# 32 bytes of padding in front of the ring of weight parts in a two-layer decoder trunk

## The chip, the cores and the metric

One core of one Trainium2 chip runs the whole program. The metric is the device time of one execution in microseconds; the kernel before was run three times, and the median counts. One further execution was taken with the hardware profiler, and all rows below come from it.

## What is computed

Two decoder layers over 256 positions of width 1024. Each layer is a mixer (latent attention in layer 0, three-branch sparse attention in layer 1), a residual with layer norm, and a PEER feed-forward with 16384 experts, again with residual and norm. Cut to the part that fills most of the time:

```python
def chunk(xc):                                   # PEER, 128 positions at a time
    q = (xc @ w_q).reshape(PEER_CHUNK, PEER_HEADS, 2, PEER_DK // 2)
    sc = jnp.einsum("thpd,hpnd->thpn", q, subkeys)
    s_half, i_half = lax.top_k(sc, PEER_TOPK)
    ...
    best, pos = lax.top_k(cand, PEER_TOPK)
    experts = jnp.take_along_axis(cand_idx, pos, axis=-1)
    g = jax.nn.softmax(best, axis=-1)
    a = jax.nn.gelu(jnp.einsum("thkd,td->thk", u[experts], xc), approximate=False)
    return jnp.einsum("thk,thkd->td", (g * a), v[experts])
```

The kernel does not gather `u`: it multiplies the activations with all 128 blocks of 128 experts, masks the result with the gates, and multiplies that with all of `v`. Only the last 64 positions (`GT`) gather their rows of `v`.

## The kernel before, in words

**Weight stream.** All weights pass through one stream (`plan`, L50) of parts of 128x1024 float32, one after the other: the latent-attention weights, then for each layer the 16 parts of `p_wq`, 128 parts of `p_u` and 128 of `p_v`, with the sparse-attention weights between the layers. A DMA from SyncE (L102 for two parts of `p_v`, L107 else) lands a part in one of four places of the tile `raw` (or, during `p_v`, in a second tile `spare` that lies where `hT` was). ScalarE rounds it to fp32r (L119, tile `hi`), VectorE subtracts (L130, tile `lo` = raw minus hi). `hi` and `lo` come from the pool `shl` of four buffers each: this is the ring of weight parts. TensorE then multiplies three products, hi with hi, hi with lo and lo with hi, so that the sum has float32's precision.

**The stages.** In the order of time:
- Latent attention (`mla`, L908). Its weights meet `hT` once (`proj_N`, L203, activations as the operand that is loaded into the array) and then `cT` (`proj_T`, L198, 256 columns streamed) and `oT` (`out_mm`, L1124, 512 columns of the weights streamed). Two of its eight output weights are kept in a pool `mkeep`, tile `keep`.
- PEER (`peer`, L442), once per layer. First 12 parts of `p_wq` by `proj_T`: the weights are loaded, 128x128 at a time, and `hT`, the transposed activations, is streamed, 256 columns at a time. Then 128 steps over `p_u` (`u_step`, L715): the first 40-odd are like `proj_T`, 24 matmuls of 256 columns. Once the routing is over, a step is "wide": 8 matmuls that stream 512 columns (both parts of `hT` side by side, for `hi`) and 8 of 256 (for `lo`), and every fourth step has 16 small fp16 matmuls from the one-hot tile `hot` beside it. Then 128 steps over `p_v` (`v_mm`, L813): here the masked activations `W` are loaded and the weight parts are streamed, 512 columns at a time, 10 matmuls a step. `W` lies in a tile of pool `r8` for steps 0 to 86 (`w_hi`, L766, takes `W[0]` as long as `late` is empty, and runs three steps ahead), and in the pool `late` (L847) for the rest.
- Sparse attention (`nsa`, L1246) between the two PEER parts: `hT` with weights by `proj_T`, and `oT` with weights by `out_mm`.

**Order.** The order of TensorE's work is written out by hand; a step's weights are prepared two steps ahead (`prep`, L157), so a step never waits for its DMA unless the ring falls behind.

**Places in memory.** Pools are stacked in the order in which they are opened (L352 to L358), and a tile takes a whole number of 32-byte units per partition. From the declared sizes follow the places of the tiles modulo 128 bytes:
- `const` starts at 0 and holds 2432 bytes and three small constants of 32 each, so `hT` (pool `pers`) starts at 96. Every further index of `hT` is a multiple of 128 bytes.
- `hT` has 16384 bytes, `small` 1088, so pool `r8` (`gb`, `hN`, the first `W`, `hot`) starts at 32; `raw`, behind its 16384 bytes, at 32; the ring `shl`, behind 16384 more, at 32. `spare` is where `hT` was, at 96.
- What is opened behind the ring: in `mla`, `cT` and `oT` are at 32 and `keep` at 64; in `peer`, the routing tiles, the gathered rows and the late `W` are at 32; in `nsa`, `oT` and its `keep` are at 96.

In this text the distance of a matmul is the place of the streamed operand minus that of the loaded one, modulo 128.

Of the kernel before, what the change touches and what calls it, by code (L numbers as in the profile page):

```python
# [12 lines left out]
F32 = mybir.dt.float32  # L13
# [11 lines left out]
P = 128  # L25
# [18 lines left out]
class Kern:  # L44
# [302 lines left out]
    def build(self):  # L347
        tc, nc, I = self.tc, self.nc, self.I
        with ExitStack() as es:
            es.enter_context(tc.manual_schedule())  # L350
            pool = lambda *a, **k: es.enter_context(tc.tile_pool(*a, **k))
# [3 lines left out]
            self.pr8 = pool(name="r8", bufs=2)  # L355
            self.nraw = 4
            self.raw4 = pool(name="sraw", bufs=1).tile([P, self.nraw, D], F32, name="raw")
            self.shl = pool(name="shl", bufs=4)  # L358
            self.pacc = pool(name="pacc", bufs=2, space=PSUM)
            self.pmm = pool(name="pmm", bufs=4, space=PSUM)  # L360
# [1303 lines left out]
```

## Time and profile before

| | us |
|---|---|
| runs | 1757.70, 1756.76, 1750.29 |
| median | 1756.76 |
| the profiled execution's own time | 1749.82 |
| its span, first to last instruction | 1748.0 |
| its mean granted TensorE clock | 0.994 |

The profile lists, by engine, busy time and shares of the span. The times that the trace gives to single matmuls overlap, since a matmul starts before the one before it has ended. What one matmul costs is read from the starts: a row of the timeline merges neighbours of one kind, and the start of the next row minus its own start, divided by its count, is the pace. The rows on which the prediction rests stand below the change.

### The profile page before, as it was taken

Reading aid. Unit: us, or ns where it says so; the run is one execution under the profiler, and the core shown is the slowest. Engines: PE = TensorE matmul, PEld = TensorE weight load, DVE = VectorE, ACT = ScalarE, POOL = GpSimd, SP = SyncE. Lnnn points to the kernel's source line nnn. Section 1 sums busy time; section 2 is a strip of 40 time slices with the busy share of each in tenths; the row PEclk is TensorE's granted clock in tenths of the full one; section 3 lists DMA queues with packets and bytes.
Section 4 is the critical chain, followed back from the end, with each engine's and each line's share of the span. In section 5 each row is a group of like instructions: output and inputs, shape, how many; then the busy total and the mean of one; then the engine's idle time right before and its main releaser. Section 6 shows DMA issues by size and latency. Waiting matters only on the chain.

```text
span 1748.0 us, 30707 instructions
## 1 busy us (share of the span) xinstructions
PE 1703.1 (97%) x10610; PEld 1478.1 (85%) x10610; DVE 1553.4 (89%) x3675; ACT 1042.9 (60%) x2267; POOL 481.4 (28%) x441
## 2 busy tenths in 40 slices
PE   7999999999999999999997999999999999999997
PEld 6879999888888788888785789998888888888886
DVE  5778988989998899999778789988899998999998
ACT  6646555766666555556466755556666666555554
POOL 2110002000001777761341210001000005777740
PEclk9999999999999999999999999999999999999999
DMA  7535667555556899999572265657555557999993
GB/s 246 169 128 195 193 204 261 186 178 181 187 183 251 309 391 370 367 360 332 179 268 67 95 206 176 205 184 275 176 181 186 184 183 290 401 383 369 361 363 110
DMA packets 118619, 416.66 MB, mean 238 GB/s; under 512 B 16032, under 2 KB 18112, under 8 KB 117376
## 3 DMA queue, kind: packets, MB, share of 16 engines
q1 hardware_dynamic: 88976, 322.60, 54.2%
q0 software_dynamic: 29488, 92.10, 14.1%
q8 instruction: 84, 1.38, 0.3%
q14 instruction: 71, 0.58, 0.1%
HBM read 400.49 MB, written 13.63 MB: 237 GB/s over the span
## 4 chain that ended last, share of the span: by engine, by line
PE 72%; issue 16%; DVE 6%; DMA 2%; ACT 2%; POOL 1%; SPq 0%; POOLq 0%; ACTq 0%; DVEq 0%
PE acc L196 36%; PE mm L196 35%; PE mm L223 1%; DVE lo L130 1%; DMA raw<-p_wq 1%; POOL actD L758 1%; DVE keep L130 1%; DMA xT<-xT 0%; POOL row L472 0%; ACT hi L119 0%; POOL gel L476 0%; DMA gel<-actD,gidx 0%; DVE gacc L486 0%; DVE W L774 0%; DMA actD<-gst 0%
## 5 line engine op out<-in xcount | busy, mean ns | idle before, releaser
L119 ACT CAST hi<-raw 128x1024 fp32r<-128x1024 f32 (+1 forms) x463 | 484.6, 1049 | 244.6 <-PE acc L196 99.8
L196 PE MATMUL mm<-hT,hi 128*128 128x256 f32 (+1 forms) x3360 | 612.8, 328 | 0.0
L130 DVE TENSOR_TENSOR lo<-raw,hi 128x1024 fp32r<-128x1024 f32 (+1 forms) x459 | 558.3, 1220 | 32.6 <-ACT hi L119 30.9
L196 PEld LDWEIGHTS mm<-hT,hi 128*128 128x128 f32 x3360 | 483.2, 188 | 46.3 <-issue 1.2
L196 PE MATMUL acc<-hi,W 128*128 128x512 f32 x1452 | 408.8, 390 | 0.0
L196 PEld LDWEIGHTS acc<-hi,W 128*128 128x128 f32 x1452 | 273.2, 188 | 57.0
L196 PEld LDWEIGHTS mm<-hT,lo 128*128 128x128 f32 x2376 | 306.7, 188 | 15.9
L196 PE MATMUL mm<-hT,lo 128*128 128x256 f32 x2376 | 320.0, 277 | 0.0
L196 PE MATMUL acc<-lo,W 128*128 128x512 f32 x968 | 299.6, 391 | 1.8 <-DVE lo L130 1.8
L758 POOL DMA_DIRECT2D actD<-gst x64 | 34.8, 544 | 783.9 <-ACT gst L756 783.9
L472 POOL DMA_INDIRECT row<-p_v,gidx x128 | 191.7, 1498 | 117.8 <-DVE gacc L486 79.9
L196 PEld LDWEIGHTS acc<-lo,W 128*128 128x128 f32 x968 | 181.7, 188 | 41.4 <-DVE lo L130 4.1
L119 ACT CAST hi<-spare 128x1024 fp32r<-128x1024 f32 x122 | 128.1, 1050 | 113.9 <-PE acc L196 100.8
L476 POOL DMA_INDIRECT gel<-actD,gidx x128 | 165.7, 1294 | 50.0 <-issue 36.6
L486 DVE SCALAR_TENSOR_TENSOR gacc<-row,gw,gacc 128x1024 f32<-128x1024 f32 x126 | 161.4, 1281 | 1.1
L130 DVE TENSOR_TENSOR lo<-spare,hi 128x1024 fp32r<-128x1024 f32 x122 | 148.8, 1220 | 5.4 <-ACT hi L119 4.5
L750 ACT ACTIVATE mm<-mm 128x192 f32<-128x192 f32 (+23 forms) x170 | 41.1, 242 | 122.4 <-DVE mm L748 122.4
L774 DVE TENSOR_TENSOR W<-A,W 128x128 fp32r<-128x128 f32 (+1 forms) x512 | 107.6, 252 | 1.8 <-ACT W L769 1.8
L748 DVE TENSOR_TENSOR mm<-mm,half 128x256 f32<-128x256 f32 x174 | 74.5, 428 | 15.4 <-ACT half L747 15.0
L769 ACT CAST W<-A 128x192 fp32r<-128x192 f32 x256 | 88.0, 345 | 0.0
L647 DVE SCALAR_TENSOR_TENSOR A<-acc,A 128x176 f32<-128x176 f32 (+16 forms) x268 | 56.1, 274 | 28.6 <-PE acc L196 25.6
L753 ACT ACTIVATE A<-mm 128x192 f32<-128x192 f32 (+23 forms) x244 | 67.3, 276 | 7.8 <-DVE mm L748 2.8
(275 smaller groups left out, 1759.1 us busy)
## 6 DMA issues: line engine op xcount, KB each, us to landing
raw<-p_u SPq DMA_DIRECT2D x256, 512.0 KB, 4.0
spare<-p_v SPq DMA_DIRECT2D x64, 1024.0 KB, 8.8
raw<-p_v SPq DMA_DIRECT2D x63, 1024.0 KB, 8.7
raw<-p_wq SPq DMA_DIRECT2D x32, 512.0 KB, 4.1
actD<-gst POOLq DMA_DIRECT2D x64, 128.0 KB, 3.9
raw<-b_wo SPq DMA_DIRECT2D x12, 512.0 KB, 3.8
raw<-a_wo SPq DMA_DIRECT2D x8, 512.0 KB, 4.6
raw<-s_wT SPq DMA_DIRECT2D x8, 512.0 KB, 5.6
```

Source lines behind the costliest of these rows:

```text
L119: self.nc.scalar.copy(self.his[i], self.raws[i])
L130: e.tensor_tensor(self.los[i], raw, self.his[i].bitcast(F32), op=OP.subtract)
L196: self.nc.tensor.matmul(out, a, b, start=start, stop=stop)
L472: nc.gpsimd.indirect_dma_start(out=t, out_offset=None, in_=gtable, in_offset=bass.IndirectOffsetOnAxis(ap=gidx[:, 0, c:c + 1], axis=0))
L476: nc.gpsimd.indirect_dma_start(out=gel[c // 4][:, c % 4:c % 4 + 1], out_offset=None, in_=gplaces, in_offset=bass.IndirectOffsetOnAxis(ap=g ...
L486: nc.vector.scalar_tensor_tensor(gacc, t, gw[:, c:c + 1], gacc, op0=OP.mult, op1=OP.add)
L647: nc.vector.scalar_tensor_tensor(y, pv[:, j0:j0 + m], 1.0 / GS, y, op0=OP.mult, op1=OP.mult)
L748: nc.vector.tensor_tensor(ps[:, 0:S], ps[:, 0:S], t, op=OP.add)
L753: nc.scalar.activation(y[:, n:ND], ps[:, n:ND], AF.Gelu)
L758: nc.gpsimd.dma_start(self.actD[:, jj - 3:jj + 1, :], gst.pop())
L769: nc.scalar.copy(WW[j][:, 0:ND], slot(j))
L774: nc.vector.tensor_tensor(WW[j][:, o:o + c.stop - c.start], slot(j)[:, c], WW[j][:, c].bitcast(F32), op=OP.subtract)
```

## The change

A tile of 8 floats per partition is placed in a pool of its own, between the pool of `raw` and the pool of the ring. Nothing reads or writes it.

```diff
             self.raw4 = pool(name="sraw", bufs=1).tile([P, self.nraw, D], F32, name="raw")
+            pool(name="pad", bufs=1).tile([P, 8], F32, name="pad")
             self.shl = pool(name="shl", bufs=4)
```

All that is opened behind it lies 32 bytes further on. The ring is then at 64 modulo 128, `hT` stays at 96, `r8`, `raw` and `spare` stay where they were, and what is opened behind the ring moves with it. No instruction is added or taken away.

## Rows read from the trace of the kernel before

**Rows 1.** The page: span, busy time of each engine, granted clock in 40 slices.
```profile
span 1748.0 us, 30707 instructions
...
PE 1703.1 (97%) x10610; PEld 1478.1 (85%) x10610; DVE 1553.4 (89%) x3675; ACT 1042.9 (60%) x2267; POOL 481.4 (28%) x441
...
PEclk9999999999999999999999999999999999999999
```

**Rows 2.** Stretches of layer 0: `p_wq` and first `p_u`, wide `p_u`, `p_v`.
```profile
core 0: us, PE busy (x) PEld busy (x) DVE busy (x) ACT busy (x) POOL busy (x), PEclk, DMA share, GB/s
150.00:262.00 112.00, 111.99 (x984) 111.80 (x983) 103.53 (x426) 60.61 (x121) 3.79 (x7) 1.00 0.62 193
330.00:520.00 190.00, 190.00 (x1283) 165.81 (x1283) 175.41 (x442) 123.25 (x347) 8.10 (x15) 1.00 0.57 181
600.00:800.00 200.00, 200.00 (x884) 165.68 (x883) 195.63 (x331) 115.17 (x178) 140.67 (x97) 1.00 0.99 372
```

**Rows 3.** Chain that ended last, longest pieces: start us, us, what.
```profile
171.92 87.77 PE mm L196 x772
...
1212.32 11.15 PE mm L196 x64
...
1453.97 251.38 PE acc L196 x1108
```

**Rows 4.** TensorE's groups by shape: operation, tiles, columns, count, busy us and mean ns.
```profile
L196 PE MATMUL acc<-hi,W 128*128 128x512 f32 x1452 | 408.8, 390 | 0.0
L196 PE MATMUL mm<-hT,hi 128*128 128x512 f32 x1392 | 364.1, 397 | 0.0
L196 PE MATMUL mm<-hT,lo 128*128 128x256 f32 x2376 | 320.0, 277 | 0.0
L196 PE MATMUL acc<-lo,W 128*128 128x512 f32 x968 | 299.6, 391 | 1.8 <-DVE lo L130 1.8
L196 PE MATMUL mm<-hT,hi 128*128 128x256 f32 x1968 | 248.6, 279 | 0.0
...
L196 PE MATMUL acc<-hi,hT 128*128 128x512 f32 x128 | 38.8, 420 | 10.8 <-ACT hi L119 7.2 <-ACT hT L305 3.4
...
L196 PE MATMUL acc<-lo,hT 128*128 128x512 f32 x64 | 18.4, 402 | 0.6 <-DVE lo L130 0.6
```

**Rows 5.** Timeline of TensorE in a narrow `p_u` stretch: start us, us, what.
```profile
198.78 1.07 PE L196 MATMUL mm<-hT,lo 128*128 128x256 f32 x8
199.69 1.98 PE L196 MATMUL mm<-hT,hi 128*128 128x256 f32 x16
201.50 1.07 PE L196 MATMUL mm<-hT,lo 128*128 128x256 f32 x8
202.41 1.98 PE L196 MATMUL mm<-hT,hi 128*128 128x256 f32 x16
204.22 1.07 PE L196 MATMUL mm<-hT,lo 128*128 128x256 f32 x8
```

**Rows 6.** The same for `mla`, latent projections with `cT`.
```profile
54.92 1.12 PE L196 MATMUL mm<-cT,hi 128*128 128x256 f32 x8
55.88 0.64 PE L196 MATMUL mm<-cT,lo 128*128 128x256 f32 x4
56.36 0.39 PE L196 MATMUL mm<-kT,qT 96*128 96x128 f32 x2
```

**Rows 7.** The same for two wide steps of `p_u`.
```profile
413.76 2.02 PE L196 MATMUL mm<-hT,hi 128*128 128x512 f32 x8
415.62 1.07 PE L196 MATMUL mm<-hT,lo 128*128 128x256 f32 x8
416.53 2.02 PE L196 MATMUL mm<-hT,hi 128*128 128x512 f32 x8
```

**Rows 8.** The same for two steps of `p_v`.
```profile
640.52 0.62 PE L196 MATMUL acc<-hi,W 128*128 128x512 f32 x2
...
645.05 0.62 PE L196 MATMUL acc<-hi,W 128*128 128x512 f32 x2
```

**Rows 9.** The same for the output projection of `mla`.
```profile
106.78 0.61 PE L196 MATMUL acc<-lo,oT 128*128 128x512 f32 x2
...
110.41 1.56 PE L196 MATMUL acc<-keep,oT 128*128 128x512 f32 x6
111.81 0.60 PE L223 MATMUL mm<-ident,hN 128*128 128x128 f32 x4
```

**Rows 10.** The same for the output projection of `nsa`.
```profile
998.65 1.10 PE L196 MATMUL acc<-hi,oT 128*128 128x512 f32 x4
...
1005.65 1.10 PE L196 MATMUL acc<-hi,oT 128*128 128x512 f32 x4
```

**Rows 11.** Rounding and subtracting from `raw` and from `spare`, by line.
```profile
L119 ACT CAST hi<-raw 128x1024 fp32r<-128x1024 f32 (+1 forms) x463 | 484.6, 1049 | 244.6 <-PE acc L196 99.8
L130 DVE TENSOR_TENSOR lo<-raw,hi 128x1024 fp32r<-128x1024 f32 (+1 forms) x459 | 558.3, 1220 | 32.6 <-ACT hi L119 30.9
...
L119 ACT CAST hi<-spare 128x1024 fp32r<-128x1024 f32 x122 | 128.1, 1050 | 113.9 <-PE acc L196 100.8
...
L130 DVE TENSOR_TENSOR lo<-spare,hi 128x1024 fp32r<-128x1024 f32 x122 | 148.8, 1220 | 5.4 <-ACT hi L119 4.5
```

## The prediction

> **What bounds the kernel now.** I read the page first: TensorE is busy 97% of the span, with the granted clock in the top tenth in every slice, so at its upper level of 2.4 GHz [rows 1]. The stretches by stage say where this holds: TensorE is busy for all of the 112 us of the narrow stretch, all of the 190 us of wide steps and all of the 200 us of `p_v`, at a granted clock of 1.00 [rows 2]. VectorE comes close behind in the last two, with 175.4 of 190 us and 195.6 of 200. The chain that ended last agrees: its longest pieces are runs of TensorE matmuls with nothing between them [rows 3]. So in these stages a nanosecond more or less per matmul goes into the time one to one, and what one matmul costs is its pace, from start to start.
>
> **The paces.** The narrow stretch starts 48 matmuls from 198.78 to 204.22 us, 113.3 ns each [rows 5]; over its long piece of the chain it is 87.77 us for 772, 113.7 ns [rows 3]. In the wide step the 512-column matmuls start every 1.86 us / 8 = 232.5 ns and the 256-column ones every 0.91 / 8 = 113.8 [rows 7]; a whole wide step is 11.15 / 4 = 2.79 us [rows 3]. In `p_v` twenty matmuls of 512 columns take 4.53 us, 226.5 ns each [rows 8], and 1108 of the chain 226.9 [rows 3].
>
> Now the distances, worked out from the places in the kernel's section. Narrow and wide steps stream `hT` (96) against the ring (32): distance 64. `p_v` streams the ring (32) against `W` (32): distance 0. Two other places give each shape at another distance. Latent projections stream 256 columns of `cT` (32) against the ring (32), distance 0, at 1.44 us / 12 = 120.0 ns [rows 6]; the sparse output projection streams 512 columns of the ring (32) against `oT` (96), distance 64, at 7.00 us / 30 = 233.3 (four and two alternate, five rounds) [rows 10]. So for equal shapes the pace does change with the place:
>
> - 256 columns: 113.3 ns at 64, 120.0 at 0.
> - 512 columns: 226.5 ns at 0, 232.5 to 233.3 at 64.
>
> The better distance for the one shape is the worse for the other, and a bad one costs some 6.7 ns a matmul. I take this for a meeting of TensorE's two reads, streamed and loaded, which settles into a fixed rhythm; the rows show the rhythm and not its mechanism.
>
> **What the change moves.** It adds no instruction, wait or DMA. Three kinds of matmul get a new distance; every count is from [rows 4].
>
> *Narrow, `hT` against the ring: 64 becomes 32.* There are 1968 + 2376 = 4344 of 256 columns. No row has this shape at 32. Bounds: 113.3 at 64, a change of (113.3 - 113.7) x 4344 = -1.7 us, and 120.0 at 0, +6.3 x 4344 = +27.4 us. 32 lies midway between both, so I take the middle of present mean and upper end, 116.85: +3.15 x 4344 = **+13.7 us**.
>
> *Wide, `hT` against the ring: 64 becomes 32.* There are 1392 of 512 columns. Here one row has the new distance: in `mla`, `keep` (64) is streamed against `oT` (32), six matmuls from 110.41 to 111.81, 233.3 ns [rows 9]. They are few, but they follow directly on a run at distance 0 that had settled at 3.63 us / 16 = 226.9 (two and four in turn), so it is the new distance that lifts them. I take 233.3: +0.8 x 1392 = **+1.1 us**. Bounds: the pace at 0, 226.7, gives -5.8 x 1392 = -8.1; twice the worst narrow pace, 240, gives +10.4.
>
> *`p_v` while `W` lies in `r8`: 0 becomes 32.* `W` stays at 32 and the streamed ring goes to 64. These are steps 0 to 86 of 128, 10 matmuls each, in two layers: 1740. The later steps have `W` behind the ring, both move, and stay at 0. The same row prices it, and even its sequel fits, a settled run at 0 and then 32: 233.3 - 226.5 = 6.8 ns, x 1740 = **+11.8 us** [rows 8, 9]. Bounds: nothing, if the rhythm settles again after more than six matmuls, and 240, +23.5. I exclude a gain, since no 512-column row runs faster than this one.
>
> *The rest.* Where `hT` is loaded and weights are streamed, the distance goes from 64 to 96: 192 matmuls of 512 columns [rows 4], at 6.7 ns either way 1.3 us; taken as nothing. `mla` after its first projection and `nsa`'s `oT` and scores move as one. ScalarE's rounding takes 1049 ns from `raw` (32) and 1050 from `spare` (96), VectorE's subtraction 1220 from both [rows 11]: they don't feel the place, and cost nothing here. If they did, VectorE would be next to bound, with 4.4 us of room in 200 of `p_v` [rows 2].
>
> **Sum.** 13.7 + 1.1 + 11.8 = 26.6 us on the profiled execution's 1749.82, so 1776.4. That execution lies 6.9 us under the median of the runs and just under their lowest; I leave the forecast at 1776 and let the range take the seven up or down. Bounds summed: -9.8 and +61.3 us.
>
> **The rivals.**
>
> *Faster.* At 32 both shapes of `hT` find their good rhythm, 113.3 and 226.7, and `p_v` settles back at 226.5 after a few matmuls. Price: -1.7 - 8.1 = -9.8 us, so 1740 on the profiled time or 1747 on the median. It decides from the wide pace: below about 228 ns, with `p_v` unchanged. For it: both good paces exist, and `p_v` shows that a run keeps one for hundreds of microseconds. Against it: the six `keep` matmuls.
>
> *No change.* Either 32 happens to be like 64 for `hT` and `p_v` recovers, or the place doesn't matter at all. The rows have 120.0 against 113.3 ns for one shape, in settled runs without an idle [rows 5, 6], which speaks against the latter. The Trainium skill ("SBUF — State Buffer", section "Who interferes with whom") gives TensorE two independent read ports and says that it never waits on anyone. By that rule the padding would do nothing and the time would be that of before; the trace disagrees by those 6.7 ns, unless something other than the place divides `cT` from `hT`. The padding tile, which nothing uses, could also be dropped, and then nothing moves. Time: 1750 to 1757.
>
> *`p_v` alone.* The `hT` paces stay and only `p_v` pays: 1749.8 + 11.8 = 1762, slower, but by little.
>
> **How the numbers follow.** A measurement of this kernel tells some 0.5% from no change, 8.8 us; the three runs alone span 7.4. Chances: the sum above, with the narrow pace anywhere over 115, 0.38; `p_v` alone 0.22, of which 0.02 falls short of 0.5%; no change 0.22 (0.15 by compensation, 0.07 because the place doesn't matter or doesn't move); faster 0.18, a little more than the one row at 32 would leave, since six matmuls are few and a pace at 32 for `hT` is unseen. That is 0.18 faster, 0.24 same, 0.58 slower. The range goes from 1745, between both ends of the faster case, to 1806, where narrow matmuls run at 120 and `p_v` between 233 and 240 (1749.8 + 27.4 + 1.1 + 17.6 = 1796, and seven to ten more for the level of the runs).
>
> **What would show it.** Right: with equal counts of instructions, the timeline of `p_v` has 20 matmuls in 4.67 us instead of 4.53 up to step 86 and in 4.53 from there on; narrow runs start every 115 to 120 ns; a wide step takes more than 2.79 us; rows with `cT` and `oT` are unchanged. Wrong: `p_v` at 226.5 throughout, or wide steps of 2.72 us (8 x 226.7 + 8 x 113.3). If ScalarE's or VectorE's means change from 1049 and 1220 ns, my account of what moves is wrong.

## The result, and the profile after

The changed kernel takes 1776.48 us (median of five runs, 1775.17 to 1778.65) beside 1755.69 of before (its five runs by now): a ratio of 1.0125, 95% interval 1.0111 to 1.0138, so 20.8 us slower. Its profiled execution took 1775.94 us, 26.1 more than the profiled one of before.

The page of the changed kernel, span, busy times and granted clock, against [rows 1]:

```profile
span 1774.2 us, 30707 instructions
...
PE 1735.1 (98%) x10610; PEld 1497.3 (84%) x10610; DVE 1556.8 (88%) x3675; ACT 1044.6 (59%) x2267; POOL 484.9 (27%) x441
...
PEclk9999999999999999999998999999999999999999
```

The counts of instructions are the same. TensorE is busy 32.0 us longer; VectorE, ScalarE and GpSimd 2 to 4 us. Rounding and subtraction, by line, against [rows 11]:

```profile
L119 ACT CAST hi<-raw 128x1024 fp32r<-128x1024 f32 (+1 forms) x463 | 483.4, 1046 | 254.6 <-PE acc L196 114.3
...
L130 DVE TENSOR_TENSOR lo<-raw,hi 128x1024 fp32r<-128x1024 f32 (+1 forms) x459 | 558.2, 1219 | 41.4 <-ACT hi L119 39.4
...
L130 DVE TENSOR_TENSOR lo<-spare,hi 128x1024 fp32r<-128x1024 f32 x122 | 148.9, 1220 | 11.3 <-ACT hi L119 10.5
```

Their means are those of before, 1046 to 1050 and 1219 to 1220 ns, though `hi` and `lo` moved and `raw` did not. They only wait a little longer, for one another and for TensorE.

The chain that ended last in the changed kernel, some long pieces (start us, us, what), against [rows 3]:

```profile
173.85 90.83 PE mm L196 x772
...
300.07 11.29 PE mm L196 x64
...
1081.07 91.85 PE mm L196 x772
...
1467.12 264.35 PE acc L196 x1140
```

The narrow piece of 772 matmuls takes 90.83 us in layer 0 and 91.85 in layer 1, where both took 87.77: 117.7 and 119.0 ns a matmul. Four wide steps take 11.29 us instead of 11.15.

The timeline of TensorE in wide steps of the changed kernel, against [rows 7]:

```profile
407.95 2.03 PE L196 MATMUL mm<-hT,hi 128*128 128x512 f32 x8
409.82 1.11 PE L196 MATMUL mm<-hT,lo 128*128 128x256 f32 x8
410.77 2.04 PE L196 MATMUL mm<-hT,hi 128*128 128x512 f32 x8
```

The 512-column matmuls start every 1.87 / 8 = 233.8 ns (232.5 before), the 256-column ones every 0.95 / 8 = 118.8 (113.8 before).

The timeline of `p_v` in the changed kernel, first with `W` in `r8`, against [rows 8], then with `W` in `late`:

```profile
638.06 0.63 PE L196 MATMUL acc<-hi,W 128*128 128x512 f32 x2
...
642.73 0.63 PE L196 MATMUL acc<-hi,W 128*128 128x512 f32 x2
...
757.06 0.63 PE L196 MATMUL acc<-hi,W 128*128 128x512 f32 x2
...
761.73 0.62 PE L196 MATMUL acc<-hi,W 128*128 128x512 f32 x2
...
766.26 0.62 PE L196 MATMUL acc<-hi,W 128*128 128x512 f32 x2
```

Twenty matmuls lie between the first two rows, 4.67 us or 233.5 ns each, and again between the next two; twenty between the last two, 4.53 us or 226.5. The matmul at 761.73 is the 871st of `p_v` in this layer: the 7 ns a matmul end with step 86, where `W` moves behind the ring. In the profile of before the pace does not change at that step.

By pace, against the profiled execution of before, the wide steps pay +0.035 us x 174 = 6.1 and `p_v` +7.0 ns x 1740 = 12.2. Stage by stage, from the start of a stage's first matmul to that of the next, the difference of the two profiles is: narrow +3.7 and +4.5 us in the two layers, wide +3.2 and +3.2, `p_v` +2.0 and +5.6, all the rest (the two attentions and what joins them to PEER) +4.0, together 26.2. Two of these are not the pace of the moved matmuls. The 4.0 us lie where the prediction took nothing; profiles with the distances of before, shown further down, spread as far there (308.6 to 313.7 us). And `p_v` of layer 0 shows 2.0 us only because the profile of before lost 3.7 there, as the second profile of that kernel further down tells: TensorE waited for `lo`, and behind the wait the granted clock was 0.67 from 575 to 580 us, part of that at its lower level of 1.2 GHz:

```profile
575.74 0.73 PE L196 MATMUL acc<-lo,W 128*128 128x512 f32 x2 [1.79 <-DVE lo L130]
```

### The profile page after: what moved, and what is told of

The parts are those of the page before. It is cut to its first block, busy times and chain, and to the rows that moved or that the text cites. A ratio compares the mean times of both kernels' runs of the same rounds, so it can differ in the third digit from the quotient of the medians.

```text
span 1774.2 us, 30707 instructions
## 1 busy us (share of the span) xinstructions
PE 1735.1 (98%) x10610; PEld 1497.3 (84%) x10610; DVE 1556.8 (88%) x3675; ACT 1044.6 (59%) x2267; POOL 484.9 (27%) x441
## 4 chain that ended last, share of the span: by engine, by line
PE 91%; DVE 4%; ACT 2%; DMA 1%; issue 1%; SPq 0%; ACTq 0%; DVEq 0%
PE mm L196 51%; PE acc L196 39%; PE mm L223 1%; DMA raw<-p_wq 1%; DVE lo L130 1%; DVE keep L130 1%; DMA xT<-xT 0%; ACT hi L119 0%; DVE gacc L487 0%; DVE W L775 0%; DVE hN L291 0%; DVE bnst L269 0%; DVE hN L273 0%; ACT p L1546 0%; DVE qs L1362 0%
## 5 line engine op out<-in xcount | busy, mean ns | idle before, releaser
L119 ACT CAST hi<-raw 128x1024 fp32r<-128x1024 f32 (+1 forms) x463 | 483.4, 1046 | 254.6 <-PE acc L196 114.3
L196 PE MATMUL mm<-hT,hi 128*128 128x256 f32 (+1 forms) x3360 | 622.1, 331 | 0.0
L130 DVE TENSOR_TENSOR lo<-raw,hi 128x1024 fp32r<-128x1024 f32 (+1 forms) x459 | 558.2, 1219 | 41.4 <-ACT hi L119 39.4
L196 PEld LDWEIGHTS mm<-hT,hi 128*128 128x128 f32 x3360 | 491.3, 189 | 46.9 <-issue 1.2
L196 PE MATMUL acc<-hi,W 128*128 128x512 f32 x1452 | 414.5, 393 | 0.0
L196 PE MATMUL mm<-hT,lo 128*128 128x256 f32 x2376 | 327.9, 280 | 0.0
L196 PEld LDWEIGHTS mm<-hT,lo 128*128 128x128 f32 x2376 | 313.5, 188 | 16.2
L119 ACT CAST hi<-spare 128x1024 fp32r<-128x1024 f32 x122 | 128.0, 1050 | 116.8 <-PE acc L196 109.5
L477 POOL DMA_INDIRECT gel<-actD,gidx x128 | 169.4, 1323 | 50.2 <-issue 36.6
L130 DVE TENSOR_TENSOR lo<-spare,hi 128x1024 fp32r<-128x1024 f32 x122 | 148.9, 1220 | 11.3 <-ACT hi L119 10.5
```

Source lines behind the costliest of these rows:

```text
L119: self.nc.scalar.copy(self.his[i], self.raws[i])
L130: e.tensor_tensor(self.los[i], raw, self.his[i].bitcast(F32), op=OP.subtract)
L196: self.nc.tensor.matmul(out, a, b, start=start, stop=stop)
L477: nc.gpsimd.indirect_dma_start(out=gel[c // 4][:, c % 4:c % 4 + 1], out_offset=None, in_=gplaces, in_offset=bass.IndirectOffsetOnAxis(ap=g ...
```

## The experiments

**The theory** is that of the prediction: the distance between the streamed and the loaded operand sets a matmul's pace. **Rivals:** the ring's own place does it; what lies behind the ring does it (gathered rows, routing tiles); the padding's size does it. All experiments but one move pools by padding alone, and no instruction changes. Each is given as a ratio to the kernel before, run beside it, since that kernel's median went from 1755.5 to 1760.1 us between them.

**One stage at a time.** In the first the padding stands in front of `small`, in the second three paddings move `hT` and the ring together and leave `r8` where it was:

```diff
+            pool(name="pad_small", bufs=1).tile([P, 8], F32, name="pad_small")
             self.small = pool(name="small", bufs=2)
```

> The padding stands in front of the small pool, so r8, raw and the ring move by 32 together: hT against the ring at distance 32 as after the change, p_v at distance 0 as before it. If the distance of the two TensorE operands decides: p_v at 226.7 ns a matmul in all steps, narrow matmuls at 117 to 119 and wide steps at 2.82 us as after the change; the time some 11 us under the changed kernel, about 1765 us (before: 1755.7, after: 1776.5). If the ring's own place (64 instead of 32) decides: p_v at 233 ns and 1776 us. If what lies behind the ring decides: 1776 us.

```diff
+            pool(name="pad_pers", bufs=1).tile([P, 8], F32, name="pad_pers")
             pers = pool(name="pers", bufs=1)
             self.small = pool(name="small", bufs=2)
+            pool(name="pad_r8", bufs=1).tile([P, 24], F32, name="pad_r8")
             self.pr8 = pool(name="r8", bufs=2)
...
+            pool(name="pad_shl", bufs=1).tile([P, 8], F32, name="pad_shl")
             self.shl = pool(name="shl", bufs=4)
```

> hT moves by 32, r8 and raw keep their place modulo 128, the ring moves by 32: hT against the ring at distance 64 as before, p_v at 32 while W lies in r8. If the distance decides: narrow matmuls at 113.3 ns and wide steps at 2.79 us as before, p_v at 233 ns up to step 86; about 11 us over the kernel before, 1767 us. If the ring's own place decides: narrow matmuls at 117 to 119 ns too, and 1776 us.

The first measured 1.0053 (1.0025 to 1.0081), the second 1.0055 (1.0033 to 1.0078); together 1.0108, not far from the change's 1.0125. Chain and `p_v` timeline of the first, `hT` alone at 32:

```profile
171.74 91.85 PE mm L196 x772
299.26 11.28 PE mm L196 x64
...
637.63 1.07 PE L196 MATMUL acc<-hi,W 128*128 128x512 f32 x4
...
642.17 1.07 PE L196 MATMUL acc<-hi,W 128*128 128x512 f32 x4
```

The narrow and wide stages are those of the change (119.0 ns, 2.82 us a step), and `p_v` is that of before: 4.54 us for twenty, 227 ns. The same of the second, `p_v` alone at 32:

```profile
173.37 91.17 PE mm L196 x772
323.28 11.09 PE mm L196 x64
...
637.78 0.63 PE L196 MATMUL acc<-lo,W 128*128 128x512 f32 x2
...
642.45 0.63 PE L196 MATMUL acc<-lo,W 128*128 128x512 f32 x2
```

`p_v` pays: 4.67 us for twenty. The ring's own place does not decide: in the first experiment and in the changed kernel the ring has moved by the same 32 bytes, and `p_v` runs at 227 in one and 233.5 in the other. But the second also missed: its wide step takes 2.77 us and not 2.79, and its narrow piece 91.17 and not 87.77 (for the narrow piece another reason is found below), though `hT` stands at 64 from the ring as before. Modulo 256 it doesn't. Between the starts of `hT` and of the ring lie three times 16384 bytes and 1088, which is 64 modulo 256, so before the change the distance of `hT` was 192 of 256; here the paddings add 128 bytes between them, and it is 64. After the change, and in the first experiment, it is 160.

**Other sizes of the padding.** With one line in front of `shl`, `[P, 16]` for 64 bytes and `[P, 24]` for 96:

> 64 bytes in front of the ring: hT against the ring at distance 0, p_v at 64 while W lies in r8. If the distance decides, by the paces at these distances elsewhere in the kernel: narrow 120.0 ns, +27 us; wide settles at 226.7 ns at best, -8 us, or stays near 233 where eight are too few to settle, 0; p_v 233.3 ns, +12 us: 1787 to 1795 us. If only an odd multiple of 32 hurts: 1756 us.

Measured 1.0080 (1.0053 to 1.0108), 1776.5 us beside 1759.9 of before: about half of what was expected. Part of the miss is the narrow term, which was counted from 113.7 ns (see below): the narrow piece takes 91.85 us, 119.0 ns (120 expected). A four-step wide piece takes 11.31 us, more than before, where the same or less was expected; `hT` is at 128 of 256. Another part is `p_v`, at 64 of 256; its timeline:

```profile
638.07 0.62 PE L196 MATMUL acc<-lo,W 128*128 128x512 f32 x2
...
642.65 0.62 PE L196 MATMUL acc<-lo,W 128*128 128x512 f32 x2
```

Twenty take 4.58 us, 229 ns, where `nsa`'s output projection, also at 64 modulo 128, takes 233.3 [rows 10]. That one is at 192 of 256.

> 96 bytes in front of the ring: hT against the ring at distance 96, which is 32 the other way round, and p_v likewise. If only the size of the distance counts, all paces are those after the change: narrow 117 to 119 ns, wide steps 2.82 us, p_v 233 ns, 1776 us. If it counts which operand lies ahead, they differ from these, narrow anywhere from 113.3 to 120 ns and p_v from 226.7 to 233: 1746 to 1795 us.

Measured 1.0147 (1.0111 to 1.0182), 1787.5 us, the slowest of all: the narrow piece takes 92.86 us, 120.3 ns, four wide steps 11.37, and `p_v` twenty matmuls in 4.66 us. For the narrow matmuls 96 (120.3 ns) is not 32 the other way round (117.7 and 119.0 after the change).

**128 or 256?** With `[P, 32]` and `[P, 64]` in front of `shl`, and with 32 bytes in front of all pools:

> 128 bytes in front of the ring: modulo 128 every distance is that of the kernel before. If the distance modulo 128 decides: all paces of before, narrow 113.3 to 114.5 ns, wide 232.7, p_v 226.7, and before's time. If it decides modulo 256: hT against the ring stands at 64 of 256, as in v_only, where narrow ran at 117.7 ns and wide at 229.5; p_v with W in r8 stands at 128 of 256, which no row shows, 227 to 233 ns; with 230 for it some 13 us over before.

> 256 bytes in front of the ring. If the distance modulo 256 (or 128) decides: all paces of before, narrow 113.3 to 114.5 ns, wide 232.7, p_v 226.7, and before's time within noise. If the padding itself hurts, by moving what lies behind the ring or by its size: slower, 8 to 25 us.

```diff
+            pool(name="pad_const", bufs=1).tile([P, 8], F32, name="pad_const")
             const = pool(name="const", bufs=1)
```

> The padding stands in front of all pools: every tile lies 32 bytes further on, every distance is that of before. If the distance decides: narrow 113.3 to 114.5 ns, wide 232.7, p_v 226.7 and before's time. If a place by itself decides (hT at 128 instead of 96 modulo 256, the ring at 192 instead of 160, as in v_only and after the change): narrow 117 to 118 ns, 15 us over before.

128 bytes cost 1.0066 (1.0044 to 1.0088); 256 bytes 1.0004 (0.9991 to 1.0018), nothing; moving everything 1.0012 (0.9998 to 1.0025), nothing that can be told. Wide steps and `p_v` with 128 bytes:

```profile
404.20 1.99 PE L196 MATMUL mm<-hT,hi 128*128 128x512 f32 x8
406.03 1.11 PE L196 MATMUL mm<-hT,lo 128*128 128x256 f32 x8
406.98 2.00 PE L196 MATMUL mm<-hT,hi 128*128 128x512 f32 x8
...
637.72 0.64 PE L196 MATMUL acc<-lo,W 128*128 128x512 f32 x2
...
642.36 0.64 PE L196 MATMUL acc<-lo,W 128*128 128x512 f32 x2
```

The wide matmuls run at 1.83 / 8 = 228.8 ns, as in the second experiment and not as before, and `p_v`, at 128 of 256, at 4.64 / 20 = 232. Modulo 128 nothing had moved here. The chain with 256 bytes:

```profile
172.94 91.17 PE mm L196 x772
321.39 11.15 PE mm L196 x64
...
1459.94 251.38 PE acc L196 x1108
```

Wide steps (11.15) and `p_v` (251.38 for 1108) are to a hundredth of a microsecond those of before [rows 3]. This and the kernel moved as a whole, where 1108 matmuls of `p_v` take 251.41 us, settle the rivals: the ring and what is behind it moved in both, in the second by the same 32 bytes as in the changed kernel, and the time did not. So the pace repeats after 256 bytes, and not after 128. One thing differs from before: the narrow piece takes 91.17 us, not 87.77, and so it does in the kernel moved as a whole:

```profile
173.45 91.17 PE mm L196 x772
...
1073.62 91.17 PE mm L196 x772
```

**The kernel before once more**, since the distance was the same in all three:

> The kernel before, unchanged, profiled once more. If the narrow stage has two rhythms at the same places and the first profile caught the quicker one: its long chain piece of 772 matmuls takes 87.77 us again (time about 1750) or 91.17 us, as in pad256 and all32 (time about 1757), with p_v at 226.7 ns and wide at 232.7 in both. If instead pad256 and all32 were slowed by their padding: 87.77 us whatever the time.

```profile
171.63 91.17 PE mm L196 x772
263.12 24.51 PE mm L196 x216
297.25 11.15 PE mm L196 x64
...
1066.18 91.17 PE mm L196 x772
1157.68 25.44 PE mm L196 x216
...
1455.78 251.38 PE acc L196 x1108
```

91.17 us, without any padding, in an execution of 1751.64 us: the narrow stage has two rhythms at one and the same distance, 113.7 and 118.1 ns, and the profile on which the prediction rests had caught the quicker in both long pieces. A rhythm belongs to a piece and not to an execution. Behind each long piece come three transposes (`ident`) and then 216 more narrow matmuls, and these took 25.44 us (117.8 ns) behind the quick piece of the first profile's layer 1, but 24.51 (113.5) behind the slow one in layer 0 here:

```profile
1067.78 87.77 PE mm L196 x772
1155.87 25.44 PE mm L196 x216
```

In the five profiles at this distance eight of the twenty such pieces have the quick rhythm and twelve the slow one; in the two at distance 64 it is one of eight, and at the other distances none. That the time goes with the long piece, 1750 or 1757, is not borne out: its slower rhythm came with 1751.64.

**The rest of the circle**, `[P, 40]`, `[P, 48]` and `[P, 56]` in front of `shl`:

> 160 bytes in front of the ring: hT against the ring at 32 of 256, p_v at 160 while W lies in r8. All odd multiples of 32 seen so far gave 512 columns 232.8 to 233.9 ns and 256 columns 117.1 to 120: expected here again, 1774 to 1788 us. If 32 and 160 differ for hT as 64 and 192 do: wide at 230 or less.

> 192 bytes in front of the ring: hT against the ring at 0 of 256, p_v at 192 while W lies in r8. If the distance modulo 256 decides, whatever the tiles: narrow 119.9 ns as with cT, wide 226.7 if eight matmuls are enough to settle and up to 233 if not, p_v 233 ns as nsa's output projection at 192: +16 (narrow, over 116) + 12 (p_v) - 8 to 0 (wide), so 1776 to 1784 us beside 1756. If the paces go with the tiles and not with the distance: anything else, p_v at 226.7 to 229 for one.

> 224 bytes in front of the ring: hT against the ring at 224 of 256, which is 32 further than before, p_v at 224 while W lies in r8. No row shows 224 for either. If only multiples of 64 are good places: narrow 117 to 120 ns, p_v 233 ns, 25 to 35 us over before. If 192 is no sharp optimum: narrow 113 to 116 and p_v 227 to 230, 0 to 10 us over before.

They measured 1.0077 (1.0052 to 1.0102), 1.0114 (1.0067 to 1.0162) and 1.0113 (1.0085 to 1.0142), the last two in two runs each. With 160 and 224 bytes the paces came as expected (narrow 117.0 and 118.7 ns, `p_v` 234 and 233.5), and the times lower: 1772.7 us where 1774 to 1788 were expected, and some 20 us over before where 25 to 35 were. With 192 bytes, chain and timelines:

```profile
174.20 92.86 PE mm L196 x772
302.96 11.22 PE mm L196 x64
...
410.18 2.00 PE L196 MATMUL mm<-hT,hi 128*128 128x512 f32 x8
412.02 1.11 PE L196 MATMUL mm<-hT,lo 128*128 128x256 f32 x8
...
637.93 0.63 PE L196 MATMUL acc<-lo,W 128*128 128x512 f32 x2
...
642.60 0.63 PE L196 MATMUL acc<-lo,W 128*128 128x512 f32 x2
```

Narrow 120.3 ns at 0, as `cT` has it [rows 6]; wide 1.84 / 8 = 230, between the settled 226.5 and 233, perhaps because runs of eight have hardly time to settle, which no run tests; `p_v` at 192 takes 233.5, as `nsa`'s output projection at 192 does. So settled paces go with the distance and not with the tiles. For `p_v`, 64 and 192 differ by 4.5 ns, and for the wide steps by 3.8 in the same sense.

All paces that the runs gave, in ns from start to start, by distance modulo 256 (narrow from the chain's piece of 772; `p_v` from twenty matmuls of a timeline; wide as the mean over all unbroken runs of eight in both layers; two numbers from two profiles):

| distance | narrow, 256 columns | `p_v`, 512 columns | wide, 512 columns | wide, 256 columns |
|---|---|---|---|---|
| 0 | 120.3 | 226.5 | 230.1 | 118.5 |
| 32 | 117.0 | 233.5 | 233.3 | 116.7 |
| 64 | 118.1 | 229 | 228.9 | 115.7, 115.3 |
| 96 | 120.3 | 233 | 233.4 | 119.9 |
| 128 | 119.0 | 232 | 232.7 | 119.2 |
| 160 | 117.7, 119.0 | 234 | 234.0, 233.8 | 117.6, 117.1 |
| 192 | 113.7, 118.1 | 233.5 | 232.7 | 114.2 |
| 224 | 118.7 | 233.5 | 232.7 | 118.4 |

**A version made from the table.** By the table only the wide `hi` parts gain from another place. The ring's `hi` tiles get 128 bytes of slack each, and a part lies at one end or the other; sixteen small tiles are joined into one to win some of the room back:

```diff
+        self.nhi, self.wide = 0, False
...
-                self.his[i] = self.shl.tile([P, self.raws[i].shape[-1]], F32R, tag="hi", name="hi")
+                t = self.shl.tile([P, D + 32], F32R, tag="hi", name="hi")
+                o = 32 * ((self.nhi % 2) ^ (self.wide and i < self.v0))
+                self.nhi += 1
+                self.his[i] = t[:, o:o + self.raws[i].shape[-1]]
...
-            gel = [gat.tile([P, 4], F32, name=f"gel{m}") for m in range(16)]
+            gels = gat.tile([P, 16, 4], F32, name="gels")
+            gel = [gels[:, m, :] for m in range(16)]
...
-                wide = len(A) > 1
+                wide = self.wide = len(A) > 1
...
+            self.wide = False
```

> The hi tiles get 128 bytes of slack each, and only for the wide steps of p_u they are written 128 bytes further on: 1328 of the 1392 wide matmuls stand at 64 of 256 instead of 192; all others stay where they were before the change. If the distance modulo 256 decides: wide 229.5 ns instead of 232.7, -4.3 us over both layers, narrow in wide steps 114.2 to 115.5 (0 to +1.8), all else as before: 2.5 to 4.3 us under before, 0.14 to 0.25%. If the distance modulo 128 decides, or a place by itself: no difference.

Its chain and two wide steps:

```profile
171.95 91.17 PE mm L200 x772
320.47 11.05 PE mm L200 x64
...
405.06 2.00 PE L200 MATMUL mm<-hT,hi 128*128 128x512 f32 x8
406.89 1.07 PE L200 MATMUL mm<-hT,lo 128*128 128x256 f32 x8
407.80 2.00 PE L200 MATMUL mm<-hT,hi 128*128 128x512 f32 x8
```

The pace follows: 228.8 ns wide, narrow left at 113.8, and 11.05 us for four steps instead of 11.15. By the chain that is 0.025 us x 174 = 4.4 us. The two wide stages as a whole, from their first matmul to the first of `p_v`, took 263.9 and 264.1 us, where both profiles of before have 265.1 in both layers: 2.2 us, half of it. The time doesn't show it: 1.000, 0.998 to 1.002. An expected gain of 0.14 to 0.25% lies at the edge of that interval; whether it reaches the end stays open. No version tried is measurably quicker than the kernel before.

## Why the prediction was right

- **Forecast and sum.** 1776 us against 1776.48, and +26.6 us against the profiled execution's +26.1. That the forecast came within a microsecond is luck. Against the median of before the loss is 20.8 us, 5.8 less than the sum, and the sum started from an execution 5.9 us under that median: the two errors cancel. Which term is too large against the median no run shows; the narrow one is the likely place, for the reason below.
- **`p_v` while `W` is in `r8`.** The prediction gave 11.8 us and 4.67 us for twenty up to step 86, 4.53 after. The rows show just that, and the second experiment shows it by itself. The row that priced it, six matmuls of `keep` against `oT` [rows 9], was a true sample.
- **Wide.** Predicted 233.3 ns, measured 233.8 in the row above and 234.0 over all runs of eight, 232.7 before: 1.2 ns x 1392 = 1.7 us beside 1.1.
- **Narrow.** The middle of two bounds, 116.85, was taken for want of a row; measured 117.7 and 119.0 in the narrow stage and, over all runs of eight in wide steps, 117.6 (the row above, 118.8, is one of the slower). In the wide steps it is a true loss: 114.2 became 117.6, 3.4 ns x 1392 = 4.7 us, and with the 1.7 of the 512 columns that is the +3.2 and +3.2 us of the two wide stages. In the narrow stages the loss against the profile that the prediction had, 8.2 us in both layers, is a loss against the quicker of two rhythms; against the kernel before profiled again it is 1.2 and 1.1 us. So the 113.7 ns from which the prediction counted was not the kernel's pace but one of its two, and of the 13.7 us only the 4.7 in the wide steps and 2.3 in the narrow stages hold against both profiles.
- **The step that was wrong** is one of its premises, which the change's description shares: the distance modulo 128. It served because the rows that it was combined with agree modulo 256 as well: `hT`, and `nsa`'s `oT`, stand at 192, `keep` and `p_v` after the change both at 32. For wide it priced `hT` by `keep`, which stands at 32 of 256, while `hT` comes to stand at 160; that this came out right is luck: both are odd multiples of 32, and all four of these have 233 to 234 in `p_v`.
- **Rivals.** Faster fell by the wide pace, which it had named as decisive. No change fell with it: the padding moves the ring, and the place matters. `p_v` alone fell by the wide steps, which pay 6.4 us against both profiles of before; for the narrow stage it was nearly right, 2.3 us in both layers, when the slower rhythm is the measure. The Trainium skill ("SBUF — State Buffer", "Who interferes with whom") gives TensorE two independent read ports and says that it never waits on anyone. By that rule, as the prediction read it, the place costs nothing; here, with the same instructions and the other engines' means unchanged, `p_v` takes 226.5 to 234 ns a matmul by the place of its operands alone, so the measurement decides against it. That it is the two ports that meet is not shown.
- **Not shown** is the mechanism. That streaming and loading meet somewhere in the memory fits the dependence on the distance, but no run separates the two reads: every matmul here has its own weight load. What sets a narrow piece into one rhythm or the other is not shown either.

## What to carry to other kernels

Where TensorE is the bound and weights are loaded for every matmul, list the places of streamed and loaded tiles modulo 256 bytes, and read each shape's pace from start to start: here 3% for 512 columns (226.5 to 234 ns in `p_v`) and 5% for the 256 of the wide steps (114.2 to 119.9) hang on it. No place is the best for both shapes: at 0 the 512 columns of `p_v` are quickest and the narrow ones slowest. Padding in front of a shared pool moves every pair that the pool takes part in, so price each pair by itself. In the narrow stage 4% hung on the rhythm at one and the same place. Before a difference of 3% is put down to a change, look whether the kernel before, profiled again, keeps its own pace.

## What the runs showed of the hardware that was not expected

- The period is 256 bytes: at 128 more, 512 columns go from 226.5 to 232 ns (`p_v`, 0 to 128) and from 232.5 to 228.8 (wide, 192 to 64); at 256 more nothing changes.
- Two settled rhythms at one distance: 87.77 or 91.17 us for the same 772 matmuls of the unchanged kernel, and 24.51 or 25.44 for the 216 behind the next three transposes, not always the same one as before them.
- Settled runs repeat to 0.01 us across kernels: 91.17 us in six profiles at distances 64 and 192, 92.86 in both at 0 and 96.
